# Six weight loads per round, issued in another order: a small expert block's gate and up loads ahead of the big block's down loads

## Chip, cores and metric

The kernel runs on one core of one Trainium2 chip. The metric is the device time of one execution in microseconds (us). The core's engines are PE (TensorE: matmuls, with weight loads shown as PEld), ACT (ScalarE), DVE (VectorE), POOL (GpSimd) and SP (SyncE, which here issues nearly all DMA transfers). Each works through a queue of its own, and instructions wait for other engines through semaphores.

## The reference, cut to what matters

Two blocks of two layers each run on 256 tokens of width 1024. Only the last stage matters here, a mixture of eight experts with a swiglu each:

```python
def swiglu(x, w_gate, w_up, w_down):
    return (jax.nn.silu(x @ w_gate) * (x @ w_up)) @ w_down
...
    for e in range(N_EXPERTS):
        y = y + combine[..., e:e + 1].astype(x.dtype) * swiglu(x, w_gate[e], w_up[e], w_down[e])
```

`w_gate` and `w_up` are 1024x3584 and `w_down` is 3584x1024, in fp32, so that the eight experts are 352 MB of weights, read once each.

## The kernel before, in words

The expert stage (`_moe`) cuts every expert into 7 blocks of 512 hidden columns. A block has six loads of 1 MiB (a 128x2048 tile): two halves each of gate, up and down. Experts at even places are **big** (128 token slots), those at odd places **small** (64 slots, the last one 32). Big and small blocks alternate: after three big ones the order is small, big, small, big, ..., and two small ones end it. I call a small block with the big one after it a **round**: 12 loads. There are 26 small blocks with a big block just ahead of them.

A big block's weights go through `weights` (L424): a 1 MiB load, a CAST on ACT that writes the rounded high half (`whi`, three buffers, L437), and a subtraction on DVE that writes the low half (L438). Both halves then go to PE. A small block's weights go through `passing` (L391): the loaded tile goes to PE as it is. Tiles come from a ring of rooms (`room`, `raw`, `xlo`, `x`, ...), taken and given back in the order of the code; every load is chained behind the one before it, so that SP issues them in the order in which `raw_unit` is called.

In a small block's step of the loop PE does the first half of gate and up (`proj_few(e, b, 0)`), then the transposes of the big block before it (`turn`), then the second half (`proj_few(e, b, 1)`), and then the big block's down product (`down`). Both halves of `proj_few` add into one PSUM tile (`mm`). ACT then copies this tile out (`act`, COPY `msg<-mm`, L1917). `turn` rounds the transposed big activations into `mh`: a CAST on ACT and a subtraction on DVE (L1940). These two are tied by hand behind the casts and subtractions of the down weights:

```python
            if (e, b) in WD:

                for a, p in zip(i, self.parted):
                    self.after(a, p)
```

`self.parted` holds the last CAST and the last subtraction of `weights`. `WD` holds the down weights of the big block, asked for in the small block's step. `ahead(3000)` raises the priority of what stands in it; a scheduler sets the order in each engine's queue from priorities and dependencies, and PE's order in this stage is tied to that of the code (`kept`).

Of the kernel before, what the change touches and what calls it, by code (L numbers as in the profile page):

```python
# [283 lines left out]
class Net:  # L284
# [1410 lines left out]
    def _moe(self, x, out):  # L1695
# [11 lines left out]
        for tb in range(2):  # L1707
            ts = slice(tb * 128, tb * 128 + 128)
            with self.ahead(5000):
# [22 lines left out]
                b = nc.vector.tensor_scalar(oh[:, tb, 0], self.c["iota"], slot[:, tb, 0:1], None, op0=ALU.is_equal)  # L1732

                for c in range(2):
# [6 lines left out]
                    if tb:  # L1741
                        self.after(i, b)
                        b = i
# [19 lines left out]
        def back(oh, dt):  # L1763

            ohf = oh.bitcast(F32) if dt is F32R else oh
            oht = self.late.tile([128, NE, T], dt, name="oht", tag="oht")
            for e in range(0, NE, 2):
                p = self.psum()
                for i in range(2):
                    for tb in range(2):  # L1770
                        t = self.tr(p[:, i * 256 + tb * 128:i * 256 + tb * 128 + 128], ohf[:, tb, e + i], self.ident)
                        self.after(t, gm)
                i = nc.scalar.copy(oht[:, e:e + 2], p.rearrange("p (e t) -> p e t", e=2))
                self.after(i, gx)
            return oht
# [84 lines left out]
        def by_place(out, v):  # L1860

            nc.vector.tensor_copy(out[:, :, 0], v[:, :, 0])
            nc.vector.tensor_tensor(m2, m[:, None].to_broadcast([128, 2, 7, 7]),
                                    v[:, :, None, 1:8].to_broadcast([128, 2, 7, 7]), op=ALU.mult)
            return nc.vector.tensor_reduce(out[:, :, 1:8], m2, axis=AX.X, op=ALU.add)
# [6 lines left out]
        def block_of(n, q, b, hf):  # L1872

            if q == 0:
                return d[n][0, b, hf]
            return d[n][bass.ds(expert[q], 1), b, hf].rearrange("e p n -> (e p) n")

        H, YD, PP, WD = {}, {}, {}, {}

        def proj(e, b, n, steps=iter(())):  # L1880

            es = slice(0, 128)
            p = self.psum()
            for hf in range(2):
                w = block_of(n, e, b, hf)
                h, lo = self.weights(w, hold=early.pop(0), pieces=range(4)) if early else self.weights(w)
                for i in range(4):
                    k, cs = hf * 4 + i, slice(i * 512, i * 512 + 512)
                    self.mm(p, gh[:, k, es], h[:, cs], start=k == 0, stop=False)
                    self.mm(p, gl[:, k, es], h[:, cs], start=False, stop=False)  # L1890
                if hf:
                    next(steps, None)
                for i in range(4):
                    k, cs = hf * 4 + i, slice(i * 512, i * 512 + 512)
                    self.mm(p, gh[:, k, es], lo[:, cs], start=False, stop=k == KC - 1)
                next(steps, None) if hf == 0 else None
            PP[e, b, n] = p

        def proj_few(e, b, hf):

            p = PP[e, b] = PP.pop((e, b)) if hf else self.psum()
            with self.ahead(3000):
                ws = [self.passing(block_of(n, e, b, hf)) for n in ("mgate", "mup")]
            m = SLOTS[e]
            n = 8 * m
            for i in range(4):
                k = hf * 4 + i
                for r in range(0, 128, m):
                    w, c = ws[r // 64], r % 64 // m * n
                    self.mm(p[r:r + m, 0:n], FX[e][:, k, 0:m], w[:, i * 512 + c:i * 512 + c + n], start=k == 0,  # L1910
                            stop=k == KC - 1, tile_position=(0, r), skip_group_check=True)

        def act(e, b):
            sg = self.xp.tile([128, 512], F32, name="msg", tag="sq", bufs=2)
            if e % 2:
                n = 8 * SLOTS[e]
                nc.scalar.copy(sg[:, 0:n], PP.pop((e, b))[:, 0:n])  # L1917
            else:
                self.after(nc.scalar.activation(sg, PP.pop((e, b, "mgate")), AF.Silu), self.parted[0])
                self.after(nc.vector.tensor_tensor(sg, sg, PP.pop((e, b, "mup")), op=ALU.mult), self.parted[1])  # L1920
            H[e, b] = sg

        def turn(e, b):
            sg = H.pop((e, b))
            pt = self.psum("t")
            m = SLOTS[e]
            for i in range(4 if m == 128 else m // 16):
                self.tr(pt[:, i * 128:i * 128 + 128], sg[:, i * 128:i * 128 + 128], self.ident)
            if e % 2:

                n, h = m // 16, 64 // m
                pv = pt[:, 0:n * 128].rearrange("p (i a m) -> p a i m", i=n, a=2)
                fs, fh = (sg[:, j * 256:j * 256 + n * 64].rearrange("p (i m) -> p i m", i=n) for j in range(2))
                nc.scalar.activation(fs, pv[:, 0], AF.Silu)
                nc.vector.tensor_tensor(fh, fs, pv[:, 1], op=ALU.mult)
                H[e, b] = [fh[:, f % n, f // n * m:f // n * m + m] for f in range(4)]
                return
            i = (7 * (e // 2) + b) % 2
            hh, hl = mh[:, i, 0], mh[:, i, 1]
            i = nc.scalar.copy(hh, pt), nc.vector.tensor_tensor(hl, pt, hh.bitcast(F32), op=ALU.subtract)  # L1940
# [4 lines that stand above are left out]
            H[e, b] = hh, hl  # L1945
# [75 lines left out]
        for n, (e, b) in enumerate(blocks):  # L2021
            if n == 2:
                for q in range(1, NE):
                    expert[q] = nc.values_load(idi[0:1, q:q + 1], engines=(mybir.EngineType.SP,), min_val=1, max_val=NE - 1)
            if n == 9:

                mc = hw.tile([128, 1], F32, name="mc")
                over = hw.tile([128, 8], F32, name="over")

                nc.vector.memset(cap[:, 0:1], 128.0)  # L2030
                nc.vector.tensor_scalar(cap[:, 1:8], rank[:, 1:8], 2.5, 64.0, op0=ALU.is_lt, op1=ALU.mult)
                nc.vector.tensor_scalar(over[:, 1:8], rank[:, 1:8], 5.5, 32.0, op0=ALU.is_lt, op1=ALU.mult)
                nc.vector.tensor_tensor(cap[:, 1:8], cap[:, 1:8], over[:, 1:8], op=ALU.add)
                nc.vector.tensor_scalar(cap[:, 1:8], cap[:, 1:8], 32.0, None, op0=ALU.add)
                nc.vector.tensor_tensor(over, cnt, cap, op=ALU.subtract)
                nc.vector.tensor_reduce(mc, over, axis=AX.X, op=ALU.max)
                nc.vector.tensor_scalar(mc, mc, 0.0, None, op0=ALU.max)
                mci = hw.tile([128, 1], I32, name="mci")
                nc.vector.tensor_copy(mci, mc)
            if n == 7:  # L2040
                oht = back(oh, F32R)
            steps = iter(())
            if e % 2 and blocks[n - 1][0] % 2 == 0:
                WD[blocks[n - 1]] = [self.weights(block_of("mdown", *blocks[n - 1], hf)) for hf in range(2)]
            if e % 2:
                proj_few(e, b, 0)
            else:
                proj(e, b, "mgate")
            if n == 1:
                mh = hw.tile([128, 2, 2, 512], F32R, name="mh", tag="mh")  # L2050
            if n:
                turn(*blocks[n - 1])
            if n + 1 == first:
                steps = gather(0, some=False)
            if e % 2:
                proj_few(e, b, 1)
            else:
                if b == 6 and e + 2 < NE:
                    steps = gather(e + 2)
                proj(e, b, "mup", steps)  # L2060
            act(e, b)
            if n < 2:

                i = by_place(qcomb, comb) if n else places(oh, qslot, range(1, NE), True)
                self.hold = self.hold[0], i, None
            if n:
                down(*blocks[n - 1], steps)
            for _ in steps:
                pass
            if n > 2 and blocks[n - 2][1] == 6:  # L2070
                scatter(blocks[n - 2][0])
            if n == len(blocks) - 5:
                gb = self.rows()
# [144 lines left out]
```

## Time and profile before

| what | value |
|---|---|
| time, median of 3 runs | 1853.82 us (1853.0 to 1855.28) |
| profiled execution, its own time | 1856.29 us |
| span of its trace | 1854.5 us |
| PE busy | 1783.7 us (96%) |
| ACT busy / DVE busy | 867.3 us (47%) / 1073.1 us (58%) |
| mean DMA rate over the span | 268 GB/s |

The shares are means over stages. The expert stage takes the last 850 us or so, and there DMA and PE are both nearly full for most of the time, so its stretches have to be read apart.

### The profile page before, as it was taken

Reading aid. Unit: us, or ns where it says so; the run is one execution under the profiler, and the core shown is the slowest. Engines: PE = TensorE matmul, PEld = TensorE weight load, DVE = VectorE, ACT = ScalarE, POOL = GpSimd, SP = SyncE. Lnnn points to the kernel's source line nnn. Section 1 sums busy time; section 2 is a strip of 40 time slices with the busy share of each in tenths; the row PEclk is TensorE's granted clock in tenths of the full one; section 3 lists DMA queues with packets and bytes.
Section 4 is the critical chain, followed back from the end, with each engine's and each line's share of the span. In section 5 each row is a group of like instructions: output and inputs, shape, how many; then the busy total and the mean of one; then the engine's idle time right before and its main releaser. Section 6 shows DMA issues by size and latency. Waiting matters only on the chain. (4 is left out here: it accounts for less than half of the span.)

```text
span 1854.5 us, 27561 instructions
## 1 busy us (share of the span) xinstructions
PE 1783.7 (96%) x11038; PEld 1351.6 (73%) x11038; DVE 1073.1 (58%) x1586; ACT 867.3 (47%) x1291; POOL 33.3 (2%) x78
## 2 busy tenths in 40 slices
PE   7999999999999999999999999999999999999984
PEld 5777788778896999888977766665656566665652
DVE  3765688757644754466437755565556565565543
ACT  3454375545553544345345545444535444444531
POOL 1000010000000000000010000000000000000000
PEclk9999999999999999989998999999999999999997
DMA  9654443234211555543028799999999999999996
GB/s 386 257 225 167 175 160 125 69 115 171 92 54 63 196 184 172 197 146 117 24 102 338 287 398 394 411 413 420 421 421 421 421 421 421 421 421 420 421 420 250
DMA packets 71175, 497.71 MB, mean 268 GB/s; under 512 B 8226, under 2 KB 9538, under 8 KB 11264
## 3 DMA queue, kind: packets, MB, share of 16 engines
q1 hardware_dynamic: 70752, 495.39, 67.8%
q8 instruction: 89, 1.46, 0.3%
q0 software_dynamic: 288, 0.48, 0.1%
q14 instruction: 46, 0.38, 0.1%
HBM read 493.81 MB, written 1.05 MB: 267 GB/s over the span
## 5 line engine op out<-in xcount | busy, mean ns | idle before, releaser
L438 DVE TENSOR_TENSOR raw<-raw,whi 128x2048 fp32r<-128x2048 f32 (+1 forms) x157 | 279.8, 1800 | 198.9 <-ACT whi L437 198.2
L437 ACT CAST whi<-raw 128x2048 fp32r<-128x2048 f32 (+1 forms) x198 | 306.6, 1570 | 160.7 <-PE mm L459 48.6
L413 PE MATMUL mm<-whi,g 128*128 128x512 f32 x896 | 227.3, 396 | 2.5 <-DVE y L2011 2.5
L413 PEld LDWEIGHTS mm<-whi,g 128*128 128x128 f32 x896 | 166.4, 189 | 38.9 <-issue 4.5
L437 ACT CAST whi<-room 128x2048 fp32r<-128x2048 f32 (+1 forms) x97 | 172.9, 1803 | 31.7 <-PE mm L413 13.5
L458 PE MATMUL mm<-xhi,whi 128*128 128x256 f32 x720 | 182.1, 288 | 0.7 <-ACT whi L437 0.7
L459 PE MATMUL mm<-xlo,whi 128*128 128x256 f32 x720 | 180.4, 286 | 0.0
L413 PE MATMUL mm<-room,fx 128*64 128x512 f32 (+1 forms) x632 | 152.1, 526 | 10.6 <-DMA room<-in_mup_dram 7.2
L458 PEld LDWEIGHTS mm<-xhi,whi 128*128 128x128 f32 x720 | 137.7, 191 | 8.1 <-issue 5.6
L459 PEld LDWEIGHTS mm<-xlo,whi 128*128 128x128 f32 x720 | 137.7, 191 | 1.5 <-issue 1.4
L438 DVE TENSOR_TENSOR room<-room,whi 128x2048 fp32r<-128x2048 f32 x47 | 107.6, 2289 | 31.7 <-ACT whi L437 29.7
L413 PE MATMUL s<-whi,mh 128*128 128x512 f32 x448 | 117.2, 404 | 0.0
L413 PEld LDWEIGHTS s<-whi,mh 128*128 128x128 f32 x448 | 82.6, 189 | 37.9 <-issue 19.9
L463 PE MATMUL mm<-xhi,raw 128*128 128x256 f32 x720 | 104.3, 285 | 0.0
L413 PE MATMUL mm<-raw,fx 128*64 128x512 f32 (+1 forms) x344 | 91.5, 508 | 6.5 <-DMA raw<-in_mup_dram 6.5
L1940 ACT CAST mh<-t 128x512 fp32r<-128x512 f32 x28 | 16.4, 585 | 169.5 <-PE t L416 169.4
L463 PEld LDWEIGHTS mm<-xhi,raw 128*128 128x128 f32 x720 | 93.6, 191 | 1.2 <-DVE cin L1219 0.9
L413 PEld LDWEIGHTS mm<-room,fx 128*64 128x64 f32 (+1 forms) x632 | 47.9, 129 | 57.4 <-issue 38.9
L438 DVE TENSOR_TENSOR raw<-room,whi 128x2048 fp32r<-128x2048 f32 x30 | 68.7, 2291 | 32.7 <-ACT whi L437 31.5
L438 DVE TENSOR_TENSOR room<-raw,whi 128x2048 fp32r<-128x2048 f32 x30 | 68.8, 2292 | 28.4 <-ACT whi L437 26.9
L1920 DVE TENSOR_TENSOR msg<-msg,mm 128x512 f32<-128x512 f32 x28 | 19.3, 688 | 100.5 <-PE mm L413 100.5
L413 PEld LDWEIGHTS mm<-raw,fx 128*64 128x64 f32 (+1 forms) x344 | 28.0, 125 | 47.6 <-issue 35.6
(590 smaller groups left out, 3264.3 us busy)
## 6 DMA issues: line engine op xcount, KB each, us to landing
room<-in_mup_dram SPq DMA_DIRECT2D x66, 1024.0 KB, 13.0
room<-in_mdown_dram SPq DMA_DIRECT2D x60, 1024.0 KB, 18.0
room<-in_mgate_dram SPq DMA_DIRECT2D x55, 1024.0 KB, 15.2
raw<-in_mdown_dram SPq DMA_DIRECT2D x41, 1024.0 KB, 17.1
raw<-in_mgate_dram SPq DMA_DIRECT2D x38, 1024.0 KB, 12.8
raw<-in_mup_dram SPq DMA_DIRECT2D x33, 1024.0 KB, 18.8
raw<-in_win_dram SPq DMA_DIRECT2D x29, 1024.0 KB, 6.4
raw<-in_din_dram SPq DMA_DIRECT2D x24, 1024.0 KB, 4.8
```

The costliest lines, as they stand in the source:

```text
L413: return self.kept(self.nc.tensor.matmul(*a, **k))
L437: a = nc.scalar.copy(h[:, v], r[:, v])
L438: b = nc.vector.tensor_tensor(lo[:, v], r[:, v], h[:, v].bitcast(F32), op=ALU.subtract)
L458: nc.tensor.matmul(out, w, xh[:, k], start=start and i == 0, stop=False)
L459: nc.tensor.matmul(out, w, xl[:, k], start=False, stop=False)
L463: nc.tensor.matmul(out, lo[:, off + i * 128:off + i * 128 + 128], xh[:, k], start=False, stop=stop and i == n - 1)
L1920: self.after(nc.vector.tensor_tensor(sg, sg, PP.pop((e, b, "mup")), op=ALU.mult), self.parted[1])
L1940: i = nc.scalar.copy(hh, pt), nc.vector.tensor_tensor(hl, pt, hh.bitcast(F32), op=ALU.subtract)
```

## The change

The four loads of a small block are now asked for ahead of the big block's two down loads, in the loop, and no longer inside `proj_few`. Nothing is computed otherwise, and no load, matmul, cast or subtraction is added or taken away.

```diff
         def proj_few(e, b, hf):
 
             p = PP[e, b] = PP.pop((e, b)) if hf else self.psum()
-            with self.ahead(3000):
-                ws = [self.passing(block_of(n, e, b, hf)) for n in ("mgate", "mup")]
+            ws = GU.pop((e, b, hf))
             m = SLOTS[e]
...
             steps = iter(())
+            if e % 2:
+
+                with self.ahead(3000):
+                    for hf in range(2):
+                        GU[e, b, hf] = [self.passing(block_of(w, e, b, hf)) for w in ("mgate", "mup")]
             if e % 2 and blocks[n - 1][0] % 2 == 0:
                 WD[blocks[n - 1]] = [self.weights(block_of("mdown", *blocks[n - 1], hf)) for hf in range(2)]
```

Lines behind L1903 move by -1 and those behind L2042 by +4, so that L1917 of before is L1916 of the change, and so on.

SP's queue, the loads of the seventh small block's step (`mdown` belongs to the big block before it; an ISA row works out the address of an expert's block). Before:

```order
L385 DMA room_11398<-in_mdown_dram 128x2048
L385 ISA
L385 DMA raw_11404<-in_mdown_dram 128x2048
L385 ISA
L385 DMA room_11411<-in_mgate_dram 128x2048
L385 ISA
L385 DMA x<-in_mup_dram 128x2048
L385 ISA
L385 DMA xlo<-in_mgate_dram 128x2048
L385 ISA
L385 DMA room_11432<-in_mup_dram 128x2048
```

With the change:

```order
L385 DMA room_11398<-in_mgate_dram 128x2048
L385 ISA
L385 DMA xlo<-in_mup_dram 128x2048
L385 ISA
L385 DMA x<-in_mgate_dram 128x2048
L385 ISA
L385 DMA raw_11404<-in_mup_dram 128x2048
L385 ISA
L385 DMA room_11406<-in_mdown_dram 128x2048
L385 ISA
L385 DMA room_11412<-in_mdown_dram 128x2048
```

The two down loads moved from the first to the last place of the six.

ACT's queue in the same step, from the casts of the down weights (`whi<-room_11398` and `whi<-raw_11404` before, `whi<-room_11406` and `whi<-room_11412` with the change) to the next big block's casts; `msg<-mm` as a COPY is the small block's copy out of PSUM, as an ACTIVATE the big block's silu, and `msg<-t` is the silu of the small block before. Before:

```order
L1934 ACTIVATE msg<-t 128x256
L1919 ACTIVATE msg<-mm 128x512
L437 CAST whi<-room_11398 128x2048
L437 CAST whi<-raw_11404 128x2048
L1940 CAST mh<-t 128x512
L1917 COPY msg<-mm 128x512
L437 CAST whi<-raw_11469 128x2048
```

With the change:

```order
L1918 ACTIVATE msg<-mm 128x512
L1933 ACTIVATE msg<-t 128x256
L1916 COPY msg<-mm 128x512
L437 CAST whi<-room_11406 128x2048
L437 CAST whi<-room_11412 128x2048
L1939 CAST mh<-t 128x512
L437 CAST whi<-room 128x2048
```

The COPY moved from behind the two down casts and the `mh` cast to ahead of them.

DVE's queue in the same step with the change (before, its three rows of the down weights and of `mh` stand in the same order):

```order
L1934 TENSOR_TENSOR msg<-msg,t 128x256
L1919 TENSOR_TENSOR msg<-msg,mm 128x512
L438 TENSOR_TENSOR raw_11409<-room_11406,whi 128x2048
L438 TENSOR_TENSOR room_11415<-room_11412,whi 128x2048
L1939 TENSOR_TENSOR mh<-t,mh 128x512
```

The subtraction of `mh` stays behind both subtractions of the down weights. PE's queue has the same matmuls in the same order as before, under other tile names.

## Rows read from the trace of the kernel before

**Rows 1.** Windows: stretch, length, busy us (x instructions) by engine, clock, DMA share, GB/s

```profile
1040.00:1220.00 180.00, 180.00 (x844) 115.21 (x843) 102.64 (x82) 83.85 (x71) 0.00 (x0) 1.00 0.93 374
1220.00:1680.00 460.00, 457.95 (x2117) 285.52 (x2115) 260.94 (x188) 209.16 (x171) 0.00 (x0) 1.00 1.01 421
1680.00:1840.00 160.00, 137.03 (x1017) 88.60 (x1019) 71.66 (x52) 58.41 (x55) 0.58 (x1) 0.95 0.97 402
```

**Rows 2.** Timeline of SP's DMA issues: start, length, what is issued

```profile
1112.26 0.34 SPq L385 DMA_DIRECT2D room<-in_mdown_dram  x1
1124.89 0.34 SPq L385 DMA_DIRECT2D room<-in_mgate_dram  x1
...
1128.78 0.33 SPq L385 DMA_DIRECT2D room<-in_mup_dram  x1
```

**Rows 3.** Timeline of ACT, DVE and PE in the fourth small block's step

```profile
1121.80 2.13 PE L413 MATMUL s<-whi,mh 128*128 128x512 f32 x8
...
1136.17 1.92 ACT L437 CAST whi<-room 128x2048 fp32r<-128x2048 f32 x1
1146.67 0.59 ACT L1940 CAST mh<-t 128x512 fp32r<-128x512 f32 x1 [8.59 <-PE t L416]
1147.29 0.69 DVE L1940 TENSOR_TENSOR mh<-t,mh 128x512 fp32r<-128x512 f32 x1 [2.88 <-ACT mh L1940]
1150.15 2.13 PE L413 MATMUL s<-whi,mh 128*128 128x512 f32 x8
1150.27 0.59 ACT L1917 COPY msg<-mm 128x512 f32<-128x512 f32 x1 [3.01 <-PE mm L413]
1150.75 3.71 ACT L437 CAST whi<-room 128x2048 fp32r<-128x2048 f32 x2
1152.69 4.68 DVE L438 TENSOR_TENSOR room<-room,whi 128x2048 fp32r<-128x2048 f32 x2 [4.70 <-ACT whi L437]
1155.87 2.00 PE L413 MATMUL mm<-whi,g 128*128 128x512 f32 x8
1157.46 2.29 DVE L438 TENSOR_TENSOR room<-raw,whi 128x2048 fp32r<-128x2048 f32 x1
```

**Rows 4.** Groups of ACT over the stage: count, busy, mean ns, idle before

```profile
L1917 ACT COPY msg<-mm 128x512 f32<-128x512 f32 x21 | 12.3, 586 | 63.2 <-PE mm L413 63.2
L1917 ACT COPY msg<-mm 128x256 f32<-128x256 f32 x7 | 2.6, 373 | 27.6 <-PE mm L413 27.6
```

**Rows 5.** Timeline of PE near the end: idle ahead of a row in brackets

```profile
1706.16 1.92 PE L413 MATMUL mm<-raw,fx 128*32 128x256 f32 x28 [1.87 <-DMA raw<-in_mup_dram]
...
1711.13 3.59 PE L413 MATMUL mm<-room,fx 128*32 128x256 f32 x28 [1.86 <-DMA room<-in_mup_dram]
...
1735.98 1.92 PE L413 MATMUL mm<-room,fx 128*32 128x256 f32 x28 [1.86 <-DMA room<-in_mup_dram]
...
1741.11 2.93 PE L413 MATMUL mm<-raw,fx 128*32 128x256 f32 x28 [2.02 <-DMA raw<-in_mup_dram]
...
1782.54 3.55 PE L413 MATMUL mm<-whi,g 128*128 128x512 f32 x8
1785.89 1.25 PE L413 MATMUL mm<-raw,g 128*128 128x512 f32 x4
1786.98 1.98 PE L413 MATMUL mm<-whi,g 128*128 128x512 f32 x8
1788.79 1.07 PE L413 MATMUL mm<-room,g 128*128 128x512 f32 x4
```

**Rows 6.** Windows with a low granted clock (columns as in rows 1)

```profile
988.00:992.00 4.00, 0.95 (x5) 0.55 (x5) 3.25 (x9) 1.94 (x4) 0.87 (x1) 0.87 1.02 420
...
1000.00:1004.00 4.00, 3.76 (x19) 3.69 (x19) 3.13 (x11) 2.70 (x5) 0.00 (x0) 0.50 1.01 422
1710.00:1714.00 4.00, 2.87 (x26) 1.36 (x28) 0.01 (x1) 0.00 (x0) 0.00 (x0) 0.64 1.01 420
1782.00:1786.00 4.00, 4.00 (x11) 2.71 (x10) 2.29 (x1) 2.29 (x3) 0.00 (x0) 0.60 1.02 418
```

More of the change, by code (lines that the diff above doesn't have):

```diff
@@ L1876, in block_of @@
             return d[n][bass.ds(expert[q], 1), b, hf].rearrange("e p n -> (e p) n")
-        H, YD, PP, WD = {}, {}, {}, {}
+        H, YD, PP, WD, GU = {}, {}, {}, {}, {}
         def proj(e, b, n, steps=iter(())):
```

## The prediction, made before the changed kernel was run

> **What bounds the kernel now.** I read the windows by stretch first, then SP's timeline, then one round's timeline of ACT, DVE and PE, and last PE's waits near the end. From 1040 to 1220 us PE has no idle time while DMA is below its best rate (374 GB/s); from 1220 to 1680 both are full (421 GB/s, PE 457.95 of 460 us); from 1680 to 1840 DMA is still full until the last load lands and PE is idle for 160 - 137.03 = 23.0 us [rows 1]. So the end comes when the last load lands, and PE is close behind for 600 us. How close: one round on PE lasts 1150.15 - 1121.80 = 28.35 us, from one big block's down product to the next [rows 3]; the 12 loads of a round are 12 x 1.0486 MB, which at 421 GB/s [rows 1] is 29.9 us. PE has 1.5 us of slack in a round where a small block has 64 slots, and no more.
>
> SP's timeline shows why DMA lost time early: after the load issued at 1112.26 SP stands still until 1124.89, and issues four loads by 1128.78 [rows 2]. By the order of the ring it waits for a room that the down product begun at 1121.80 [rows 3] gives back, and rooms that `proj_few` had given back before that stand behind it.
>
> In a round of before, ACT casts the down weights long before they are needed (the second cast starts at 1136.17) and `mh` at 1146.67, and only then waits for the second half of `proj_few`: the COPY begins at 1150.27, after 3.01 us of waiting [rows 3]. PE goes from that half straight into the down product at 1150.15, without a gap. The COPY waits for PE in this way in all 28 small blocks, 63.2 + 27.6 = 90.8 us in all [rows 4].
>
> **What the change moves.** *On SP* nothing is added: six loads per round in another order, which is now the order of use and the order in which the rooms come free. Taken alone this fills the holes of the early stretch. From 1040 to 1220 the rate is 374 instead of 421, a loss of 180 x (1 - 374/421) = 20 us of DMA time [rows 1], the most that this part can give.
>
> *On ACT* the order changes too, and that decides. In 21 of the 26 small blocks that follow a big one, the queue of the change has the COPY ahead of both casts of the down weights and ahead of the cast of `mh`; in 4 (the third small block, and the three whose step begins behind the gathering for the next big expert) it stands between the two casts; in the first nothing changes. The COPY waits for the last matmul of `proj_few`, and PE's next instruction in its unchanged order is the down product, which needs what now stands behind the COPY. That ACT does not go past a waiting instruction is in the trace: the two casts behind the COPY start at 1150.75, 0.48 us after it, though ACT had stood idle for 3.01 us [rows 3].
>
> The stall of a full round, laid out on the clock of the same step, where PE is done with `proj_few` at 1150.15 [rows 3]:
> - COPY starts 1150.27; the two casts behind it 1150.75 to 1154.46 (two casts take 3.71 us, as these do); cast of `mh` 0.59 us, done at 1155.05. PE's first down matmul can start there.
> - DVE: two subtractions 1152.69 to 1157.37 (4.68 us), then, with the gap that the next one shows (1157.46), the subtraction of `mh`, 0.69 us, done at 1158.15. By `self.parted` it stays behind both. PE's second matmul needs it.
> - Before, the second matmul started a matmul later than 1150.15, and 8 take 2.13 us, so at 1150.42. The stall is 1158.15 - 1150.42 = **7.7 us**, in two pieces: 4.9 us with no matmul, one matmul, then 3 us.
>
> With 32 slots the COPY takes 373 ns and not 586 [rows 4]: 7.5 us. In the 4 blocks with one cast behind the COPY: cast from 1150.75 to 1152.66, subtraction to 1154.98, `mh` to 1155.75, stall 1155.75 - 1150.42 = 5.3 us.
>
> *The clock.* A stall is paid again when TensorE's clock falls from 2.4 to 1.2 GHz. Of four waits of about 1.9 us, two were followed by half speed: 28 matmuls took 1.92 us behind two, 3.59 and 2.93 us behind the others [rows 5], and the granted clock is 0.64 there [rows 6]. At 1782 the twelve matmuls took 3.55 + 1.25 us where the next twelve took 1.98 + 1.07 [rows 5], 1.75 us lost. I take 1.7 us per stall. No row has a wait as long as 4.9 us in this stage; the nearest is 988 to 992, with 0.95 us of work in 4, and the clock is at half up to 1004 though PE is nearly full again [rows 6]. So I charge all 25 stalls. The bounds are 0 (the clock holds) and 5.7 us (the whole down product, 1150.15 to 1155.87 [rows 3], at half speed, as the windows up to 1004 would have it [rows 6]).
> The Trainium skill, TensorE: Matmul & The Clock Gate, section "HAM oscillation", tells of a kernel in which every short batch waited for its data and every one started at the low clock. By it all 25 stalls pay, 25 x 1.7 = 42 us; by the two of four waits in this trace, half of that, 21 us less. My sum stands on the first, since the stalls here are longer than those waits.
>
> *Sum.* 16 rounds with 64 slots x (7.7 + 1.7) = 150.4; 5 with 32 slots x (7.5 + 1.7) = 46.0; 4 x (5.3 + 1.7) = 28.0; together 224.4 us on PE. The cover is gone at once: with 28.35 + 9.4 = 37.8 us a round PE is slower than the 29.9 us of the loads, so the ring stays full and PE is the bound to the end. That gives back PE's waits for loads near the end: 23.0 us [rows 1], of which I leave 4 us to the last block's own chain (copy, transposes, silu, down), and the half-speed losses at 1711 and 1741, about 1.7 + 1.6 us [rows 5], which those rounds now pay anyway: 19.0 + 3.3 = 22.3 us. Net 224.4 - 22.3 = +202 us. What is late next: the next big block's casts run during the stalled down product, one of the three `whi` buffers being free at once, so no second stall follows in the round. The profiled execution took 1856.29 us for a span of 1854.5, and lies 2.5 us above the median of the runs: 1856.3 + 202.1 = 2058.4 profiled, **2056 us** as a median.
>
> **Rivals.**
> - *The DMA order is all that counts (faster).* If the down casts still ran before the COPY, the 20 us lost by DMA in the early stretch would come back and the end, which follows the last load, with them: 1854 - 20 = 1834 us. For it: SP's hole of 12.6 us [rows 2], and the burst behind it. Against it: ACT's queue. It decides below 20 / 25 = 0.8 us of stall per round; the worked one is ten times that.
> - *The stall hides behind DMA (no change).* PE's slack of 1.5 us per round would cover a stall of that size, and the time would stay at 1854 us. The stall is 7.7 us by rows of this very step.
> - *PE waits for ACT alone and the clock holds.* Without the DVE part a full stall is 1155.05 - 1150.15 = 4.9 us, a partial one 3.1: 16 x 4.9 + 5 x 4.7 + 4 x 3.1 = 114, less 19 given back, +95: 1949 us. Against it: the low half of `mh` is tied behind the subtractions. With the DVE part and a steady clock: 224.4 - 42.5 - 19 = +163: 2017 us.
> - *Half speed for the whole down product.* 4.0 us more in 25 rounds, +100: 2156 us. For it the window at 1000 to 1004 [rows 6]; against it the recovery within some 3.5 us at 1711 and 1782 [rows 5].
>
> **How the numbers follow.** My forecast, stalls of 7.7 us with a clock cost between none and twice mine (2017 to 2100 us), gets 0.74; half speed for much longer 0.08; a stall without DVE's part 0.11; the faster rival 0.05; no change 0.02. The range that leaves out about 2 in 10 goes from 1985, between the rival without DVE's part and the steady clock, to 2115, with some of the longer half speed. A measurement of this kernel can tell about 0.2% from no change, 4 us. The cases give slower 0.93, within 0.2% 0.02, faster 0.05.
>
> **What would show it.** The COPY of `msg` on ACT directly ahead of the down weights' casts, and those without idle time; the first matmul of each down product idle for about 5 us until ACT, then about 3 us until DVE; 8 down matmuls at over 3 us instead of 2.13; rounds of about 38 us; a DMA rate near 333 GB/s in the middle (12.58 MB in 37.8 us), with SP waiting for rooms; next to no PE wait for loads near the end. I am wrong if PE enters the down product without a gap, if DVE's low half of `mh` is there before the casts, or if the loads stay the bound at 421 GB/s.

## The result, and the profile after

The changed kernel takes **2052.74 us** (median of 4 runs, 2051.39 to 2054.03) against 1854.55 us for the kernel before on the same chips: a ratio of 1.1068, 95% interval 1.1049 to 1.1087. That is +198 us, where +202 was forecast (2056 us as a median), and inside the range.

The page of the change: its row of busy times (share of the span, instructions), then its DMA lines in 40 slices. Each digit is a tenth of full DMA use, and the last line is the rate:

```profile
span 2049.5 us, 27684 instructions
...
PE 1834.2 (89%) x11038; PEld 1388.2 (68%) x11038; DVE 1071.5 (52%) x1586; ACT 865.7 (42%) x1291; POOL 33.3 (2%) x78
...
DMA  9655441342135554403788888889878888879885
GB/s 389 231 199 213 158 138 66 124 156 83 63 106 183 185 185 156 144 24 138 324 337 331 317 322 322 326 313 342 327 292 341 334 306 327 336 297 357 346 336 238
```

In the expert stage, which begins at about slice 19, no slice comes near the 421 GB/s of before. Windows of the change, which answer to [rows 1] (the columns are the same; the stage is longer, so one window is added):

```profile
1040.00:1220.00 180.00, 155.78 (x683) 99.56 (x682) 78.88 (x64) 66.78 (x57) 0.00 (x0) 0.91 0.86 320
1220.00:1680.00 460.00, 375.90 (x1573) 231.75 (x1572) 197.82 (x141) 156.91 (x128) 0.00 (x0) 0.89 0.86 326
1680.00:1840.00 160.00, 133.96 (x561) 84.56 (x561) 69.22 (x55) 55.30 (x47) 0.00 (x0) 0.88 0.84 316
1840.00:2020.00 180.00, 145.01 (x933) 101.15 (x935) 78.83 (x52) 65.60 (x57) 0.58 (x1) 0.87 0.90 347
```

In the middle PE now has 84 of 460 us without work, where it had 2, and DMA falls from 421 to 326 GB/s: neither is full, which is what a chain between engines looks like. The granted clock falls from 1.00 to about 0.89. Where the chain lies, the timeline of the fourth small block's step in the change shows, the step of [rows 3]:

```profile
1159.17 3.65 PE L413 MATMUL mm<-raw,fx 128*64 128x512 f32 x16
...
1162.89 0.59 ACT L1916 COPY msg<-mm 128x512 f32<-128x512 f32 x1 [16.28 <-PE mm L413]
1163.38 1.90 ACT L437 CAST whi<-room 128x2048 fp32r<-128x2048 f32 x1
1165.17 1.90 ACT L437 CAST whi<-raw 128x2048 fp32r<-128x2048 f32 x1
1165.31 2.29 DVE L438 TENSOR_TENSOR raw<-room,whi 128x2048 fp32r<-128x2048 f32 x1 [12.95 <-ACT whi L437]
1166.97 0.59 ACT L1939 CAST mh<-t 128x512 fp32r<-128x512 f32 x1
...
1167.61 0.49 PE L413 MATMUL s<-whi,mh 128*128 128x512 f32 x1 [4.79 <-ACT mh L1939]
1167.69 2.29 DVE L438 TENSOR_TENSOR room<-raw,whi 128x2048 fp32r<-128x2048 f32 x1
1169.90 0.68 DVE L1939 TENSOR_TENSOR mh<-t,mh 128x512 fp32r<-128x512 f32 x1
...
1170.64 3.36 PE L413 MATMUL s<-whi,mh 128*128 128x512 f32 x7 [2.53 <-DVE mh L1939]
1173.79 1.60 PE L413 MATMUL s<-raw,mh 128*128 128x512 f32 x4
```

Read it from the COPY. ACT stood idle for 16.28 us until the second half of `proj_few` was done, with both down casts behind the COPY; they follow it without a gap, then comes `mh`. PE's first down matmul waits 4.79 us for ACT, its second 2.53 us for DVE, and the next seven take 3.36 us, where eight took 2.13 [rows 3]. The waits of the whole stage say that each of the 25 rounds has both pieces (us in total, times, longest):

```profile
PE s L413 <- ACT mh L1939: 111.7, 25, 4.8
PE s L413 <- DVE mh L1939: 56.3, 25, 2.5
```

These 168.0 us are nearly all of PE's waits there. And the clock behind the stall of this round, by windows:

```profile
1166.00:1171.00 5.00, 0.85 (x2) 0.55 (x3) 4.91 (x4) 3.36 (x3) 0.00 (x0) 0.71 1.01 424
1171.00:1175.00 4.00, 4.00 (x10) 3.13 (x10) 1.78 (x1) 0.97 (x1) 0.00 (x0) 0.51 0.17 72
1175.00:1179.00 4.00, 4.00 (x19) 3.25 (x18) 2.29 (x1) 2.64 (x2) 0.00 (x0) 1.00 0.67 215
```

0.51 is the lower of its two levels, 1.2 GHz, and it comes after 5 us with 0.85 us of work on PE; from 1175 on it is back at 2.4 GHz. So it goes in every round: in all 25 stalled down products the seven matmuls behind the second wait take 3.35 or 3.36 us, also in the four with one cast ahead of the COPY, where the waits are shorter. One of those:

```profile
1207.99 0.50 PE L413 MATMUL s<-whi,mh 128*128 128x512 f32 x1 [3.00 <-ACT mh L1939]
1210.43 3.35 PE L413 MATMUL s<-whi,mh 128*128 128x512 f32 x7 [1.94 <-DVE mh L1939]
```

### The profile page after: what moved, and what is told of

It is laid out like the page before. It is cut to its first block, busy times and chain, and to the rows that moved or that the text cites. A ratio compares the mean times of both kernels' runs of the same rounds, so it can differ in the third digit from the quotient of the medians.

```text
span 2049.5 us, 27684 instructions
## 1 busy us (share of the span) xinstructions
PE 1834.2 (89%) x11038; PEld 1388.2 (68%) x11038; DVE 1071.5 (52%) x1586; ACT 865.7 (42%) x1291; POOL 33.3 (2%) x78
## 5 line engine op out<-in xcount | busy, mean ns | idle before, releaser
L438 DVE TENSOR_TENSOR raw<-raw,whi 128x2048 fp32r<-128x2048 f32 (+1 forms) x166 | 300.3, 1825 | 198.3 <-ACT whi L437 198.0
L413 PE MATMUL s<-whi,mh 128*128 128x512 f32 x448 | 167.3, 520 | 168.0 <-ACT mh L1939 111.7
L413 PEld LDWEIGHTS s<-whi,mh 128*128 128x128 f32 x448 | 111.0, 255 | 224.9 <-ACT mh L1939 131.7
L437 ACT CAST whi<-room 128x2048 fp32r<-128x2048 f32 (+1 forms) x100 | 179.2, 1804 | 114.4 <-PE s L413 90.1
L413 PEld LDWEIGHTS mm<-whi,g 128*128 128x128 f32 x896 | 167.0, 190 | 38.4 <-ACT whi L437 2.6
L438 DVE TENSOR_TENSOR room<-room,whi 128x2048 fp32r<-128x2048 f32 x53 | 121.3, 2290 | 130.2 <-ACT whi L437 129.4
L1916 ACT COPY msg<-mm 128x512 f32<-128x512 f32 (+1 forms) x28 | 14.9, 532 | 331.6 <-PE mm L413 331.6
L413 PE MATMUL mm<-room,fx 128*64 128x512 f32 (+1 forms) x640 | 124.7, 489 | 0.0
L413 PEld LDWEIGHTS mm<-room,fx 128*64 128x64 f32 (+1 forms) x640 | 41.0, 123 | 64.8 <-issue 58.1
L438 DVE TENSOR_TENSOR room<-raw,whi 128x2048 fp32r<-128x2048 f32 x19 | 43.5, 2292 | 52.4 <-ACT whi L437 52.1
L413 PE MATMUL mm<-room,g 128*128 128x512 f32 x220 | 60.0, 395 | 0.0
```

The lines of the kernel that those rows point to most:

```text
L413: return self.kept(self.nc.tensor.matmul(*a, **k))
L437: a = nc.scalar.copy(h[:, v], r[:, v])
L438: b = nc.vector.tensor_tensor(lo[:, v], r[:, v], h[:, v].bitcast(F32), op=ALU.subtract)
```

## The experiments

The theory: ACT's queue order, with the COPY ahead of the down casts, is the whole loss, in two pieces (7.7 us of waiting per round through ACT, DVE and the tie of `mh`, and the clock). The main rival: the other order of the loads costs PE time by itself.

**1. The change, with ACT's queue put back** (`e1_copy_last`):

```diff
                 for a, p in zip(i, self.parted):
                     self.after(a, p)
+                self.rounded = i[0]
...
-                nc.scalar.copy(sg[:, 0:n], PP.pop((e, b))[:, 0:n])
+                i = nc.scalar.copy(sg[:, 0:n], PP.pop((e, b))[:, 0:n])
+                self.after(i, self.rounded)
+                self.rounded = None
```

> The loads in the order of the change, and on ACT the small block's COPY tied behind the cast of mh, so that ACT's queue is that of before. If ACT's queue is the whole cause (theory), PE enters each down product without a wait and the loads' better order is left alone: between 1834 us (all 20 us of the early DMA holes come back) and 1854 us (none). If the order of the loads itself costs PE time (rival), it stays near 2050 us.

Measured: 1851.05 us, 0.9976 of before (0.9967 to 0.9984). The whole loss is gone, and with it the rival. The order of the loads alone makes the kernel 0.24% faster, 4 us and not 20; that is small, but "no change" lies outside the interval.

**2. The converse: the loads as before, ACT's queue as in the change** (`e4_act_order_alone`). `firsts` keeps the last two casts of `weights`, and `rounded` the cast of `mh`:

```diff
+                self.late_casts = self.firsts if n > 3 else []
...
-                nc.scalar.copy(sg[:, 0:n], PP.pop((e, b))[:, 0:n])
+                i = nc.scalar.copy(sg[:, 0:n], PP.pop((e, b))[:, 0:n])
+                for c in self.late_casts:
+                    self.after(c, i)
+                self.late_casts = []
...
                 a = nc.scalar.copy(h[:, v], r[:, v])
+                self.after(a, getattr(self, "rounded", None))
+                self.rounded = None
```

> The kernel before with its own order of loads; the two down casts are tied behind the small block's COPY, and the next big block's first cast behind mh, so that ACT's queue is that of the change (both casts behind the COPY in 25 blocks). Theory: the same stalls of 7.7 us and the same clock cost, 2050 to 2075 us (the four blocks that had one cast ahead now pay in full, about 10 us). If the order of the loads is needed for the loss (rival), near 1855 us.

Measured: 2065.74 us, 1.1135 (1.1117 to 1.1153). The kernel before, with no load moved, loses what the change loses and 13 us more. PE's waits in its stage:

```profile
PE s L413 <- ACT mh L1946: 118.3, 25, 4.8
PE s L413 <- DVE mh L1946: 57.4, 25, 2.5
```

They are 175.7 us against 168.0: the four blocks in which the change has one cast ahead of the COPY pay in full here, 7.7 us of the 13. Some 4 more would be what the old order of the loads costs by experiment 1; these were not shown apart.

**3. The change without the tie of `mh`** (`e2_no_tie`):

```diff
-            if (e, b) in WD:
-
-                for a, p in zip(i, self.parted):
-                    self.after(a, p)
             H[e, b] = hh, hl
```

> The change without the tie of mh behind the casts and subtractions of the down weights: mh is ready early, the two down casts still stand behind the COPY. Theory: PE's first down matmul waits for one cast alone, 2.5 us, and the first low half costs 0.2 us more; 21 rounds x 2.7 = 57 us, less 22 given back, and 0 to 1.7 us of clock per round: 1890 to 1925 us. If the two down casts alone make the stall (rival), it stays above 2000 us.

Measured: 1917.52 us, 1.0341 (1.0325 to 1.0357). PE's waits in its stage:

```profile
PE s L413 <- ACT whi L437: 61.8, 25, 2.5
PE s L413 <- DVE room L438: 1.7, 9, 0.2
```

The wait is 2.5 us a round, one COPY and one cast, as worked out. So the COPY ahead of the casts makes a third of the loss (62 of 198 us), and the tie, which had been harmless while the casts ran early, the rest: a longer wait, and a clock that falls behind it every time. Behind the shorter wait it falls in some rounds only; the first twelve matmuls of two down products in this kernel's timeline:

```profile
1126.46 3.61 PE L413 MATMUL s<-whi,mh 128*128 128x512 f32 x8 [2.51 <-ACT whi L437]
1129.86 1.22 PE L413 MATMUL s<-room,mh 128*128 128x512 f32 x4
...
1196.11 2.14 PE L413 MATMUL s<-whi,mh 128*128 128x512 f32 x8 [2.51 <-ACT whi L437]
1198.43 1.20 PE L413 MATMUL s<-room,mh 128*128 128x512 f32 x4 [0.19 <-DVE room L438]
```

and the granted clock of these two stretches (0.54 and 1.00, the third number from the right):

```profile
1126.40:1130.00 3.60, 3.54 (x9) 2.75 (x10) 3.47 (x2) 3.60 (x3) 0.00 (x0) 0.54 0.94 316
1196.00:1200.00 4.00, 3.71 (x15) 2.72 (x16) 3.82 (x2) 3.67 (x3) 0.00 (x0) 1.00 0.94 336
```

Behind the same wait of 2.51 us the eight matmuls once take 3.61 us and once 2.14, as they do with no wait at all. Over the 25 rounds, the whole down product (5.7 us without a wait) takes 7.1 to 7.4 us in 14 and 6.2 to 6.3 us in 11, so a round pays about 1.1 us for the clock or nothing.

**4. The change with PE kept busy in the stall** (`e5_filled_stall`). `idle(k)` issues k matmuls of 512 columns on the resident tile `g` into a PSUM tile that nothing reads:

```diff
+                if e % 2 and n > 3 and blocks[n - 1][0] % 2 == 0:
+                    idle(16)
                 down(*blocks[n - 1], steps)
...
+                                if self.fill:
+                                    idle(8)
                                 self.mm(yd[c], hl[:, fs], h[:, ws], start=False, stop=False)
```

> The change, with 16 matmuls of 512 columns that nobody reads ahead of the first matmul of each stalled down product and 8 behind it, so that PE is busy for most of the wait. Theory: the wait stays as long, but the clock stays at its upper level, so 25 x 1.7 = 42 us come back: 2005 to 2020 us. If the clock costs nothing (rival), 2053 us; if the half-speed stretches cost 5.7 us each, 1950 us or less.

Measured: 2003.0 us, 1.0804 (1.0787 to 1.0821), 49.7 us less than the change, though PE has 600 matmuls more. A round of it on PE:

```profile
1161.42 3.92 PE L413 MATMUL mm<-g 128*128 128x512 f32 x16
1166.29 0.50 PE L413 MATMUL s<-whi,mh 128*128 128x512 f32 x1 [0.95 <-ACT mh L1939]
1166.63 2.00 PE L413 MATMUL mm<-g 128*128 128x512 f32 x8
1169.32 1.91 PE L413 MATMUL s<-whi,mh 128*128 128x512 f32 x7 [0.69 <-DVE mh L1939]
1171.07 1.09 PE L413 MATMUL s<-raw,mh 128*128 128x512 f32 x4
```

The stall is as long as in the change: from the first down matmul to the second 1169.32 - 1166.29 = 3.03 us, there 1170.64 - 1167.61 = 3.03. But seven down matmuls take 1.91 us and not 3.36, and the four behind them 1.09 and not 1.60. The clock is 49.7 / 25 = 2.0 us per round. In three of the 25 rounds the idle matmuls last longer than the wait that they fill, so this is rather too low (each of the two waits for `mh` is counted 22 times here). The granted clock stays at its upper level, where the change has 0.89 (from 1220 to 1640 us):

```profile
1220.00:1640.00 420.00, 402.73 (x1798) 255.05 (x1798) 186.91 (x134) 147.63 (x118) 0.00 (x0) 1.00 0.90 341
```

**5 and 6. Where the expected 20 us of the load order went.** In experiment 1 two things stood out. SP waited 15.1 us for the expert numbers (`values_load`), now ahead of two loads that don't need them, and after 1680 PE had three stalls, 3.0 to 4.7 us of waiting each, since the down loads now land last:

```profile
PE s L413 <- ACT mh L1941: 6.2, 3, 3.1
PE s L413 <- DVE mh L1941: 6.1, 3, 2.5
```

One run takes each of the two away. The first small block keeps its old order (`e6_first_step_old`):

```diff
+            if n == 3:
+                WD[blocks[n - 1]] = [self.weights(block_of("mdown", *blocks[n - 1], hf)) for hf in range(2)]
             if e % 2:
...
-            if e % 2 and blocks[n - 1][0] % 2 == 0:
+            if e % 2 and n > 3 and blocks[n - 1][0] % 2 == 0:
```

> As the run with the COPY tied last, but the first small block keeps the old order of its six loads, so that SP does not wait for the expert numbers ahead of two loads that don't need them (a wait of 15.1 us on SP in that run; 193 GB/s from 1000 to 1020 against 228 before). Theory (a DMA hole early in the stage is paid at the end, since the last load sets it): 35 x 20 / 421 = 1.7 us come back, 1849 us. If that hole is refilled anyway while PE is the bound (rival), 1851 us, no change against that run.

and `mh` is not tied, with the COPY behind the second down cast (`e7_no_tie_copy_last`):

```diff
             if (e, b) in WD:
 
-                for a, p in zip(i, self.parted):
-                    self.after(a, p)
-                self.rounded = i[0]
+                self.rounded = self.parted[0]
```

> As the run with the COPY tied last, but mh is not tied to the down weights, and the COPY stands behind the second down cast. In that run PE still had three stalls of about 5 us after 1680, where the down loads now land last and mh stands behind their casts. Theory: the end there follows the last load, not PE, so these stalls cost nothing and the time stays at 1851 us (1849 to 1853). If the stalls near the end are what is left of the expected 20 us (rival), up to 12 us come back: 1839 us.

Measured: 1850.80 us, 0.9977 (0.9966 to 0.9987), and 1849.91 us, 0.9977 (0.9965 to 0.9989). Neither differs from experiment 1 by more than the interval. The expected 1.7 us of the first is less than the interval (about 2 us to either side), so that rival stays open; the rival of the second, up to 12 us, is out: near the end the last load sets the time, not PE. The traces say so too. The issue of the last weight load in the kernel before and in experiments 1, 5 and 6:

```profile
1816.08 0.33 SPq L385 DMA_DIRECT2D room<-in_mdown_dram  x1
1812.35 0.33 SPq L385 DMA_DIRECT2D room<-in_mdown_dram  x1
1808.40 0.33 SPq L385 DMA_DIRECT2D room<-in_mdown_dram  x1
1807.96 0.33 SPq L385 DMA_DIRECT2D room<-in_mdown_dram  x1
```

The spans end at 1854.5, 1850.9, 1848.1 and 1846.7 us, 38.4, 38.6, 39.7 and 38.7 us behind it, whether PE stalls on the way or not.

What is left is the early stretch. Windows of experiment 1, beside [rows 1]:

```profile
1040.00:1220.00 180.00, 180.00 (x844) 115.14 (x843) 102.62 (x83) 83.20 (x70) 0.00 (x0) 1.00 0.98 390
1220.00:1680.00 460.00, 457.95 (x2094) 285.85 (x2096) 260.10 (x187) 208.15 (x168) 0.00 (x0) 1.00 1.01 421
```

and SP's waits from 1040 to 1220, first two rows of the kernel before, then three of experiment 1:

```profile
SPq L385 <- PE s L413: 78.7, 14, 12.1
SPq L385 <- PE mm L413: 46.0, 18, 5.3
...
SPq L385 <- PE mm L413: 98.7, 34, 5.2
SPq L385 <- PE s L413: 29.4, 12, 4.9
SPq L385 <- PE o L413: 14.6, 10, 2.5
```

The rate there rises from 374 to 390 GB/s, worth 180 x 16 / 421 = 6.8 us, of the 20 us up to 421. The long wait behind the down product is gone (the longest is 4.9 us, and was 12.1). But SP waits for PE as long as before in sum, 142.7 us against 140.0 (with 15.3 for `o`), now for `proj_few` and the gate and up products (98.7 against 46.0). PE is at 180 of 180 us in both kernels. A better order spreads the waits; it doesn't make PE give rooms back faster. That the 6.8 us come out as 4 at the end has a part in the windows just ahead of this stretch, the kernel before first:

```profile
960.00:980.00 20.00, 19.16 (x95) 14.29 (x95) 7.51 (x16) 4.83 (x16) 1.46 (x2) 1.00 0.53 211
960.00:980.00 20.00, 19.16 (x97) 13.93 (x96) 6.79 (x14) 6.53 (x18) 1.01 (x1) 1.00 0.43 170
```

There experiment 1 moves less, 20 x 41 / 421 = 1.9 us of loading at the best rate. Where the rest goes is open.

## Why the prediction was right

*What bounds it.* The reading of before held: PE is close behind the loads, and a stall of 7.7 us made PE's chain the bound. The slack of 1.5 us is that of a round like the one in [rows 3]. Others are longer, up to 32.6 us; seven in a row, from one of these down products to the other,

```profile
1213.38 2.13 PE L413 MATMUL s<-whi,mh 128*128 128x512 f32 x8
...
1420.96 2.13 PE L413 MATMUL s<-whi,mh 128*128 128x512 f32 x8
```

take 207.6 us, 29.65 each, which leaves 0.2 us beside the 29.9 of the loads. The forecast doesn't change by that. After 1055 us the only waits of PE in the change over 1.5 us in sum are the two rows of `mh`, and none is for a load: its waits for loads near the end are gone, as the give-back had it.

*The stall.* In the round shown the second down matmul starts at 1170.64, and the COPY, which began 0.12 us behind PE's free moment in [rows 3], at 1162.89: 1170.64 - 1162.77 - 0.27 = 7.6 us, forecast 7.7. The split, forecast 4.9 and 3, is 4.79 and 2.53 us of idle time with a slow matmul of 0.49 between. The blocks with one cast ahead show 3.00 and 1.94.

*The clock.* Forecast 1.7 us per stall, charged to all 25. All 25 paid, as the seven matmuls at 3.35 or 3.36 us show. The price was too small: experiment 4 gives 2.0, and the round shown agrees: (3.36 - 7/8 x 2.13) + (1.60 - 1.10) = 2.0, at least 0.3 us x 25 = 8 us in all. The bound of 5.7 us was far off, since the clock is back within the down product. The case that the Trainium skill tells of (TensorE: Matmul & The Clock Gate, section "HAM oscillation"), in which every wait was followed by the low clock, was a better guide to these stalls than the trace's two waits of four. For the shorter waits of experiment 3 it was not: 14 of 25 paid.

*The sum.* Forecast +202, measured +195.0 by the spans (2049.5 - 1854.5) and +198.2 by the medians. On the two pages PE is busy 50.5 us longer (1834.2 against 1783.7), about the price of the clock, and without work 144.5 us longer (span less busy time: 215.3 against 70.8). The new waits are 168.0 us, so 23.5 us of the idle time of before are gone, of which 19.0 were forecast. Two terms were off in opposite directions: the stalls were forecast at 224.4 - 42.5 = 181.9 us and show 168.0 us of waits, with a slow matmul between the two of each round; the clock was forecast at 42.5 us and cost 49.7. That the total came within 4 us is in part luck.

*The faster rival* had the right sign for the load order, and the wrong size: 20 us were to come back, 4 did (experiments 1, 5 and 6). That the end follows the last load held: 38.4 to 39.7 us lie between the two in four kernels. The step that fails is that the time lost by DMA "would come back": it took DMA's holes for time that a better order can fill, though the same window showed PE full.

## What to carry to other kernels

Moving a load in the code can move every instruction that a scheduler hangs on it; print each engine's queue before and after, and look for an instruction that waits for PE and now stands ahead of work that PE needs next. A tie made by hand (here `mh` behind the casts) costs nothing while what it is tied to runs early, and makes the largest part of the loss when that runs late (experiments 6 and 3). Where a transfer's holes and a full engine stand in the same window, don't count on the holes: here a better order of the transfers gave 4 us of the 20. Of the three versions with the COPY kept last, any gives the 0.2% that the new load order has to give.

## What was not expected of the hardware

Whether the clock falls depends on the wait, and not only on whether there is one. Behind waits of 4.6 to 4.8 and 2.2 to 2.5 us with one matmul between, and of 3.0 and 1.9 us in four rounds, it fell in all 25 rounds, and cost 2.0 us a round on average. Behind a single wait of 2.3 to 2.5 us it fell in 14 of 25, for about 1.1 us each (experiment 3). PE can be kept at its upper level through a stall by matmuls that nobody reads: 24 of them per round gained 49.7 us.
